# Output gate and z block of each head as a pair with seven-product chunks; the first convolution tap on ScalarE

## The chip, the cores and the metric

The kernel runs on one core of a Trainium2 chip. The metric is the device time of one execution in microseconds, lower is better; before the change it is 1030.87 us, the median of 3 runs from 1030.67 to 1031.13 us.

A core has a matrix engine (TensorE, in the profile PE, with its weight loads as PEld), a vector engine (VectorE, DVE), a scalar engine (ScalarE, ACT), GpSimd (POOL) and SyncE (SP), which here issues the transfers. Each engine takes its instructions in a fixed order and stops at one that waits for a semaphore. Matmuls accumulate in PSUM banks; all other tiles are in SBUF.

## The reference

One residual layer (D = 2048, 256 tokens) with two branches: a bidirectional mLSTM of 4 heads and a bidirectional RG-LRU of 16 blocks. Cut to what the change touches:

```python
# mLSTM branch: q, k, v, o, z are column blocks of one projection of the normalised input
h = h_fwd + h_bwd
h = h * rsqrt(mean(h * h, axis=-1, keepdims=True) + NORM_EPS)
h = h * head_g * sigmoid(o_p) * silu(z_p)

# RG-LRU branch, on the convolution xc (4 taps, 2 to the left) of another column block
r = sigmoid(einsum('bsnc,ncd->bsnd', xb, w_r) + b_r)
i = sigmoid(einsum('bsnc,ncd->bsnd', xb, w_i) + b_i)
a = exp(-LRU_C * r * softplus(-lam))
u = sqrt(-expm1(2.0 * log_a)) * (i * xc)     # then h_t = a_t h_(t-1) + u_t, both ways
```

Both branches are projected to D, merged by sigmoid gates of the input, and projected once more.

## The kernel before

**Numbers.** Every float32 operand x is split into two: a rounded part hi (type fp32r, ACT's cast) and the rest lo = x - hi (DVE). A product is hi·hi + hi·lo + lo·hi, three matmuls.

**Weights.** The weights come in chunks of 128 x 1024 (two rows of tiles of 128, 512 columns each; 512 KB). `load_chunk` (L106) gets a `raw` tile (5 buffers) by a transfer on SP, casts it to `whi` on ACT (L124) and writes `wlo` on DVE (L125), with 4 buffers of `whi` and of `wlo`. `block_nat` (L128) multiplies a block of 512 columns: 8 chunks of 12 matmuls (L139 to L141) into two PSUM banks `acc`. `half_tr` (L268) does half of a block with the result transposed, 4 chunks each with 8 matmuls of 512 columns (L275) and 8 of 256 (L278).

**Pairs.** `pair` (L144), in before used by four later stages, does two column blocks at once. In the chunks listed in `kqs` it replaces the eight block products by seven (Strassen's, in the form of Winograd): `products` (L166) fetches two raw tiles r1 and r2, which the host has stored as sums' parts, makes on DVE the differences t1 (L175, L176) and t2 (L180, L181), splits r1's first half (tile b), t1, t2 and r2 (L160, L161), and issues 21 matmuls in place of 24. The other operand needs a "form", `make_form` (L233): sums of blocks of the activations, split again. The partial results p1, p5, p7, p6 stand in the four `aux` banks, two more pairs of banks are `acc`. After the last product chunk they are joined (L220 to L224), the plain chunks follow, first all of block 0 and then all of block 1 (L225 to L228), each ends with an addition of its `acc` (L230) and an epilogue.

**Heads.** The program runs `rg_block(j)` and `head(j)` for j = 0 to 3 and then the ZB block, four more halves of the same kind as in `rg_block`, and the later stages. `rg_block(j)` (L633) does two `half_tr`, the fold of the result into `xp`, the convolution of 4 channels' groups (L649 first tap, L652 the other three, on DVE), the split of its result into xh (L655) and xl (L656), and puts the LRU's work on a queue. `unit` (L665) is one group's gates in one direction: 6 matmuls with 256 columns into an `aux` bank, two sigmoids (L677), i·xc (L679), a tanh (L681). `decay` (L689) has the 4 exps of a direction, `root` (L697) the two square roots, `scan` (L702) two 1024-wide operations (L704, L705) and four scans (L709 or L711), in direction 1 also the sum (L714).

`head(h)` (L726) does block V (split to vhi and vlo, L733 and L734), block O with a sigmoid from PSUM (L740), block Z with a sigmoid and a product (L745, L746) and the product of both (L747); then `mix` (L753), the product with the mLSTM's weights and the normalisation (L765, L768), and `fin` (L771), four transposes and a split (L782, L783), go on a second queue.

**Order.** Each chunk begins with `tick()` (L89), which takes one entry from each queue: an entry None is a chunk without extra work. So the lists at L716 to L722 and L786 say how many chunks lie between two pieces of work. Within that the tile scheduler orders each engine's instructions by priority; `urgent()` puts loads, casts and evacuations ahead of the rest, and `issue_after` holds a step behind a named instruction.

**Tables on ACT.** ACT loads a table when the function changes from one group to another (rows ACT_TABLE_LOAD); casts and Square need none of their own.

Of the kernel before, what the change touches and what calls it, by code (L numbers as in the profile page):

```python
# [25 lines left out]

S_WB, S_GB, S_GA, S_WA = [((0, 4), (0, 4))] * 4
S_WO = (0, 4)

# [9 lines left out]
def hybrid_encoder(ctx: ExitStack, tc: tile.TileContext, x, xt, pk, bif, fg, wg, wi, wr, wa, wb, wo, out):  # L39
# [12 lines left out]
    def name(n):  # L52
        uid[0] += 1
        return f"{n}_{uid[0]}"
# [88 lines left out]

    def pair(src, xhi, xlo, forms, kqs, dst, b11, epilogue):  # L144
        aps = [aux(i) for i in range(4)]
        p1, p5, p7, p6 = aps
        accs = [acc_pair()[1] for _ in range(2)]
        banks = [[v[:, :NB], v[:, NB:]] for v in accs]
        (d11, d21), (d12, d22) = [(v[:, :NB], v[:, NB:]) for v in dst]
        began = set()  # L150
# [15 lines left out]
        def products(kq, last):  # L166
            lf, rt_ = slice(0, NB), slice(NB, 2 * NB)
            with urgent():
                r1, r2 = [wp.tile([P, KC * NB], F32, tag="raw", name=name("raw"), bufs=5) for _ in range(2)]
                sp.dma_start(r1, src[0][kq])  # L170
                sp.dma_start(r2, src[1][kq])
                b = b11()
                split(b[:, lf], b[:, rt_], r1[:, lf])
                t1 = hp.tile([P, 2 * NB], F32, tag="vhi", name=name("t1"))
# [4 lines left out]
                t2 = hp.tile([P, 2 * NB], F32, tag="vlo", name=name("t2"))  # L179
# [12 lines left out]
            def sf(i):  # L192
                return fm[:, i * P:(i + 1) * P], fm[:, NB + i * P:NB + (i + 1) * P]

            mm(p1, *xb(0, 0), b[:, lf], b[:, rt_], last)
# [17 lines left out]
        for kq in range(last + 1):  # L213
            if kq in kqs:
                products(kq, kq == last)
            else:
                plain(kq, 0)
                plain(kq, 1)
        with urgent():
# [12 lines left out]

    def make_form(fm, full=None, parts=None):  # L233
        u = hp.tile([P, 2 * NB], F32, tag="vhi", name=name("sf"))
        if full is None:
# [397 lines left out]
    def rg_block(j):  # L633
# [31 lines left out]
        def unit(d, n):  # L665
# [10 lines left out]
            for i, v in ((0, av[d]), (1, iv[d])):  # L676
                act.activation(v[:, r], gp[:, i * S:(i + 1) * S], AF.Sigmoid,  # L677
                               bias=pks[:, PK_BRG + d * 2 + i, c:c + 1])
            dve.tensor_mul(iv[d][:, r], iv[d][:, r], xc[:, r])  # L679
            dc = d * KT + c  # L680
            st["a"] = act.activation(tv[d][:, r], av[d][:, r], AF.Tanh, scale=c4[:, dc:dc + 1]).ins  # L681
# [42 lines left out]
    yas = {}  # L724

    def head(h):  # L726
# [8 lines left out]
        to = hp.tile([P, 2 * NB], F32, tag="to", name=name("to"))  # L735
        zz = hp.tile([P, 2 * NB], F32, tag="zz", name=name("zz"))
        ps = block_nat(wi[BLK_O + h], hhi, hlo)
        with urgent():
            for tb in range(2):
                act.activation(to[:, tb * NB:(tb + 1) * NB], ps[tb], AF.Sigmoid)  # L740
        ps = block_nat(wi[BLK_Z + h], hhi, hlo)
        with urgent():
            for tb in range(2):
                v = zz[:, tb * NB:(tb + 1) * NB]
                act.activation(v, ps[tb], AF.Sigmoid)  # L745
                dve.tensor_mul(v, v, ps[tb])  # L746
        dve.tensor_mul(zz, zz, to)  # L747
        sq = hp.tile([P, 2], F32, tag="sq", name=name("sq"), bufs=2)
        if h == 0:
            yas["h"], yas["l"] = sl("A", F32R), sl("B", F32R)  # L750
        yah, yal = yas["h"], yas["l"]

        def mix(tb):  # L753
            num = aux()
# [46 lines left out]
    def h_form(kq, i):  # L801
        h4 = hl_t[:, kq * 4 * S:(kq + 1) * 4 * S].rearrange("p (k q s) -> p k q s", q=2, s=S)
        form("h", kq, i, parts=[h4[:, :, q, :] for q in range(2)])

# [34 lines left out]
    def b11():  # L839
        nb11[0] += 1  # L840
        return hp.tile([P, 2 * NB], F32R, tag=("to", "zz")[nb11[0] % 2], name=name("b11"))

# [129 lines left out]

def _pairs(c, j, kqs):
    for kq in kqs:
        u, v = c[j, kq].copy(), c[j + 1, kq].copy()
        c[j, kq] = np.concatenate([u[:, :NB], v[:, :NB]], axis=1)
        c[j + 1, kq] = np.concatenate([v[:, NB:], u[:, NB:]], axis=1)

# [46 lines left out]
```

## Time and profile before

| | before |
|---|---|
| median of 3 runs | 1030.87 us (1030.67 to 1031.13) |
| profiled run, its span | 1030.37 us, 1028.6 us |
| span outside the profile's first and last instruction | 1.8 us |
| PE busy | 1019.5 us, 99% |
| DVE busy | 786.2 us, 76% |
| ACT busy | 580.1 us, 56% |
| granted clock of PE, mean | 0.998 |
| transfers | 199.32 MB, mean 194 GB/s |

The profiled run is within 0.05% of the median. In the rows of a timeline the first number is the start in microseconds from the first instruction, the second how long the instruction or the run of equal instructions took; matmuls overlap, so their spacing, not their length, is what one costs. In brackets stands the idle time ahead of a row and what ended it. The part "releaser" of such rows is inferred from semaphores.

### The profile page before, as it was taken

Reading aid. Unit: us, or ns where it says so; the run is one execution under the profiler, and the core shown is the slowest. Engines: PE = TensorE matmul, PEld = TensorE weight load, DVE = VectorE, ACT = ScalarE, POOL = GpSimd, SP = SyncE. Lnnn points to the kernel's source line nnn. Section 1 sums busy time; section 2 is a strip of 40 time slices with the busy share of each in tenths; the row PEclk is TensorE's granted clock in tenths of the full one; section 3 lists DMA queues with packets and bytes.
Section 4 is the critical chain, followed back from the end, with each engine's and each line's share of the span. In section 5 each row is a group of like instructions: output and inputs, shape, how many; then the busy total and the mean of one; then the engine's idle time right before and its main releaser. Section 6 shows DMA issues by size and latency. Waiting matters only on the chain.

```text
span 1028.6 us, 13664 instructions
## 1 busy us (share of the span) xinstructions
PE 1019.5 (99%) x5124; PEld 867.3 (84%) x5124; DVE 786.2 (76%) x1039; ACT 580.1 (56%) x763; POOL 11.3 (1%) x35
## 2 busy tenths in 40 slices
PE   9999999999999999999999999999999999999997
PEld 9988888888888888888888888888888888888886
DVE  6787797596578649854977778887787877979784
ACT  7545457745765585559455555545554555454562
POOL 1000000000000000000000000000000000000000
PEclk9999999999999999999999999999999999999999
DMA  9654445554555555554655455555566645666562
GB/s 349 255 188 140 164 162 177 175 203 167 182 201 187 183 179 180 191 190 156 212 184 187 163 203 197 211 209 183 194 204 208 214 167 206 212 244 255 183 205 82
DMA packets 55954, 199.32 MB, mean 194 GB/s; under 512 B 6352, under 2 KB 6864, under 8 KB 55504
## 3 DMA queue, kind: packets, MB, share of 16 engines
q1 hardware_dynamic: 55024, 197.13, 55.1%
q10 hardware_dynamic: 864, 1.32, 0.4%
q8 instruction: 40, 0.66, 0.3%
q14 instruction: 26, 0.21, 0.1%
HBM read 196.33 MB, written 2.10 MB: 193 GB/s over the span
## 4 chain that ended last, share of the span: by engine, by line
PE 98%; DMA 1%; DVE 0%; SPq 0%; ACT 0%; issue 0%; DVEq 0%
PE acc L275 16%; PE acc L157 11%; PE acc L154 11%; PE acc L156 11%; PE acc L139 9%; PE acc L140 9%; PE acc L141 9%; PE acc L278 8%; PE aux L154 2%; PE aux L157 2%; PE aux L156 2%; PE aux L761 1%; PE aux L675 1%; PE aux L674 1%; PE aux L673 1%; PE aux L951 1%
## 5 line engine op out<-in xcount | busy, mean ns | idle before, releaser
L125 DVE TENSOR_TENSOR wlo<-raw,whi 128x1024 fp32r<-128x1024 f32 (+1 forms) x321 | 389.3, 1219 | 154.6 <-ACT whi L124 152.6
L124 ACT CAST whi<-raw 128x1024 fp32r<-128x1024 f32 (+1 forms) x321 | 334.4, 1048 | 267.7 <-PE acc L141 80.9
L275 PE MATMUL acc<-sHL,whi 128*128 128x512 f32 x704 | 178.6, 394 | 0.0
L139 PE MATMUL acc<-whi,sHL 128*128 128x512 f32 x416 | 162.4, 390 | 0.0
L140 PE MATMUL acc<-wlo,sHL 128*128 128x512 f32 x416 | 162.2, 390 | 0.0
L141 PE MATMUL acc<-whi,sHL 128*128 128x512 f32 x416 | 162.0, 389 | 0.0
L275 PEld LDWEIGHTS acc<-sHL,whi 128*128 128x128 f32 x704 | 127.0, 189 | 23.7
L278 PEld LDWEIGHTS acc<-sHL,wlo 128*128 128x128 f32 x704 | 96.1, 190 | 7.2
L156 PE MATMUL acc<-wlo,sHL 128*128 128x512 f32 x260 | 101.1, 389 | 0.0
L157 PE MATMUL acc<-whi,sHL 128*128 128x512 f32 x260 | 101.1, 389 | 0.0
L154 PE MATMUL acc<-whi,sHL 128*128 128x512 f32 x260 | 99.5, 389 | 0.0
L278 PE MATMUL acc<-sHL,wlo 128*128 128x256 f32 x704 | 99.2, 283 | 0.0
L141 PEld LDWEIGHTS acc<-whi,sHL 128*128 128x128 f32 x416 | 78.1, 188 | 16.3
L139 PEld LDWEIGHTS acc<-whi,sHL 128*128 128x128 f32 x416 | 78.2, 188 | 15.6
L140 PEld LDWEIGHTS acc<-wlo,sHL 128*128 128x128 f32 x416 | 78.2, 188 | 15.3
L160 ACT CAST whi<-t 128x1024 fp32r<-128x1024 f32 x36 | 37.9, 1053 | 57.4 <-PE acc L157 41.2
L157 PEld LDWEIGHTS acc<-whi,sHL 128*128 128x128 f32 x260 | 48.8, 188 | 10.2
L156 PEld LDWEIGHTS acc<-wlo,sHL 128*128 128x128 f32 x260 | 48.8, 188 | 10.2
L154 PEld LDWEIGHTS acc<-whi,sHL 128*128 128x128 f32 x260 | 48.8, 188 | 10.1
L161 DVE TENSOR_TENSOR wlo<-t,whi 128x1024 fp32r<-128x1024 f32 x36 | 44.0, 1223 | 14.6 <-ACT whi L160 14.6
L156 PE MATMUL acc<-wlo,sA 128*128 128x512 f32 x104 | 40.6, 390 | 0.0
L157 PE MATMUL acc<-whi,sB 128*128 128x512 f32 x104 | 40.5, 390 | 0.0
(314 smaller groups left out, 1435.2 us busy)
## 6 DMA issues: line engine op xcount, KB each, us to landing
raw<-wi SPq DMA_DIRECT2D x255, 512.0 KB, 3.6
raw<-wb SPq DMA_DIRECT2D x32, 512.0 KB, 3.7
raw<-wa SPq DMA_DIRECT2D x32, 512.0 KB, 3.7
raw<-wo SPq DMA_DIRECT2D x32, 512.0 KB, 4.4
raw<-wr SPq DMA_DIRECT2D x8, 512.0 KB, 3.6
sB<-x SPq DMA_DIRECT2D x4, 512.0 KB, 8.3
sA<-x SPq DMA_DIRECT2D x1, 2048.0 KB, 7.4
sA<-xt SPq DMA_DIRECT2D x7, 256.0 KB, 7.2
```

The costliest lines, as they stand in the source:

```text
L124: last_copy[0] = act.copy(hi[:, r], raw[:, r]).ins
L125: last_sub[0] = dve.tensor_sub(lo[:, r], raw[:, r], f(hi[:, r])).ins
L139: pe.matmul(ps[tb], a, wh, start=(k == 0), stop=False)
L140: pe.matmul(ps[tb], a, wl, start=False, stop=False)
L141: pe.matmul(ps[tb], b, wh, start=False, stop=(k == KT - 1))
L154: pe.matmul(ps, a, wh, start=id(ps) not in began, stop=False)
L156: pe.matmul(ps, a, wl, start=False, stop=False)
L157: pe.matmul(ps, b, wh, start=False, stop=stop)
L160: act.copy(hi, v)
L161: dve.tensor_sub(lo, v, f(hi))
L275: pe.matmul(ps[m], hi[:, o:o + P], hl_t[:, 2 * k * S:2 * (k + 1) * S], start=(k == 0), stop=False, skip_group_check=True)
L278: pe.matmul(ps[m][:, :S], lo[:, o:o + P], hhi(k * S, (k + 1) * S), start=False, stop=(k == KT - 1), skip_group_check=True)
```

## The change

1. In `head`, blocks O and Z are done by `pair`, with product chunks 0, 2 and 4 in heads 0, 1 and 2, and 0 and 2 in head 3 (`S_OZ`); the other chunks are plain. t1 and t2 use the tiles of `to` and `zz`. The sigmoids and products of O and Z become the epilogue `epi_oz`, on whole tiles in SBUF: sigmoid(o) when block O is done; when Z is done, o·z, sigmoid(z) and their product.
2. The three forms of the input that this needs are made once, in head 0, ahead of its block V; they lie in free parts of the tiles that later hold the head outputs. Tile b has a place of its own.
3. The convolution's first tap is an ACT activation with scale and bias. xl is written by one subtraction over 1024 columns, after all four groups; i·xc by one product a direction, after its second pair of units.
4. The LRU's queue entries are fewer: the units of direction 1 and the decays, root and scans have other due chunks.
5. On the host the columns of O and Z are stored as the pair needs them; the number of bytes is the same.

```diff
+S_OZ = ((0, 2, 4), (0, 2, 4), (0, 2, 4), (0, 2))
...
-    def pair(src, xhi, xlo, forms, kqs, dst, b11, epilogue):
+    def pair(src, xhi, xlo, forms, kqs, dst, b11, epilogue, tmp=("vhi", "vlo")):
...
-            dve.tensor_scalar(v, xp[:, n, 0:S], pks[:, PK_CW, c:c + 1], pks[:, PK_CB, c:c + 1],
-                              op0=ALU.mult, op1=ALU.add)
+            act.activation(v, xp[:, n, 0:S], AF.Identity, scale=pks[:, PK_CW, c:c + 1], bias=pks[:, PK_CB, c:c + 1])
...
             act.copy(xh[:, r], v)
-            dve.tensor_sub(xl[:, r], v, f(xh[:, r]))
+        dve.tensor_sub(xl, xc, f(xh))
...
-            dve.tensor_mul(iv[d][:, r], iv[d][:, r], xc[:, r])
...
             unit(d, 2 * half + 1)
+            if half:
+                dve.tensor_mul(iv[d], iv[d], xc)
...
-            queue.extend([None] * (5 if d == 0 else 4))
+            queue.extend([None] * (5 if d == 0 else 1))
             for half in range(2):
                 queue.append(lambda d=d, half=half: gates(d, half))
-        queue.extend([None, None])
-        queue.extend([lambda: decay(0), None, lambda: decay(1), None, root, None, None, lambda: scan(0), None,
-                      lambda: scan(1)])
+        queue.extend([None, lambda: decay(0), lambda: decay(1), root, None, lambda: scan(0), None, lambda: scan(1)])
...
+        if h == 0:
+            yas["h"], yas["l"] = sl("A", F32R), sl("B", F32R)
+            for kq, (t, i) in ((0, ("h", 3)), (2, ("l", 3)), (4, ("h", 2))):
+                hf[kq] = yas[t][:, i * 1024:(i + 1) * 1024]
+                make_form(hf[kq], parts=h_parts(kq), tag="to" if kq % 4 else "zz")
...
-        ps = block_nat(wi[BLK_O + h], hhi, hlo)
-        with urgent():
-            for tb in range(2):
-                act.activation(to[:, tb * NB:(tb + 1) * NB], ps[tb], AF.Sigmoid)
-        ps = block_nat(wi[BLK_Z + h], hhi, hlo)
-        with urgent():
-            for tb in range(2):
-                v = zz[:, tb * NB:(tb + 1) * NB]
-                act.activation(v, ps[tb], AF.Sigmoid)
-                dve.tensor_mul(v, v, ps[tb])
-        dve.tensor_mul(zz, zz, to)
+        def epi_oz(jj):
+            to, zz = dst
+            if jj == 0:
+                act.activation(to, to, AF.Sigmoid)
+            else:
+                dve.tensor_mul(to, to, zz)
+                act.activation(zz, zz, AF.Sigmoid)
+                dve.tensor_mul(zz, zz, to)
...
+        pair((wi[BLK_O + h], wi[BLK_Z + h]), hhi, hlo, hf, S_OZ[h], dst, b11, epi_oz, tmp=("to", "zz"))
```

The order of the instructions moves with it. Three places follow; the names carry running numbers (whi_2962 is one buffer's use), and in the changed kernel the lines are later by one to fifteen: casts L125, wlo L126, gates L679 (sigmoid) and L682 (tanh), exp L697, root L703, scan L707, L708, L712, L714.

ACT in head 1, before, from the last gate unit of direction 1 to the first cast behind the sigmoid of block O:

```order
L124 CAST whi_2774<-raw_2773 128x1024
L677 ACTIVATE sC_468_2385<-aux_2704,pks 128x256
L677 ACTIVATE sC_470_2387<-aux_2704,pks 128x256
L681 ACTIVATE sD_471_2388<-sC_468_2385,c_175 128x256 x2
L694 ACT_TABLE_LOAD
L694 ACTIVATE sC_467_2384<-sC_467_2384,c_174 128x256 x4
L124 CAST whi_2795<-raw_2794 128x1024
L694 ACTIVATE sC_468_2385<-sC_468_2385,c_174 128x256 x4
L124 CAST whi_2817<-raw_2816 128x1024
L124 CAST whi_2835<-raw_2834 128x1024
L700 ACT_TABLE_LOAD
L700 ACTIVATE sE_1520<-sE_1520 128x1024
```

The same place of ACT in the changed kernel, from the load for the exps; the last unit's sigmoids (on aux_2898) stand behind it:

```order
L697 ACT_TABLE_LOAD
L697 ACTIVATE sC_484_2431<-sC_484_2431,c_174 128x256 x4
L697 ACTIVATE sC_485_2432<-sC_485_2432,c_174 128x256 x3
L125 CAST whi_2984<-raw_2983 128x1024
L703 ACT_TABLE_LOAD
L703 ACTIVATE sE_1520<-sE_1520 128x1024
L125 CAST whi_3004<-raw_3003 128x1024
L679 ACT_TABLE_LOAD
L679 ACTIVATE sC_485_2432<-aux_2898,pks 128x256
L679 ACTIVATE sC_487_2434<-aux_2898,pks 128x256
L125 CAST whi_3028<-raw_3027 128x1024
L682 ACTIVATE sD_488_2435<-sC_485_2432,c_175 128x256
```

Seven of the eight exps and the first root run ahead of the last unit, so behind its tanh come the sigmoid of O, a load and the eighth exp, a load and the second root, and a load for the sigmoid of Z.

DVE at the transition from head 1 to the RG block of head 2, changed kernel, from the first scan step:

```order
L707 SCALAR_TENSOR_TENSOR sE_1520<-sC_484_2431,sE_1520 128x1024
L126 TENSOR_TENSOR wlo_3068<-raw_3066,whi_3067 128x1024
L708 TENSOR_TENSOR sE_1520<-sE_1520,sC_486_2433 128x1024
L126 TENSOR_TENSOR wlo_3101<-raw_3099,whi_3100 128x1024
L707 SCALAR_TENSOR_TENSOR sD_488_2435<-sC_485_2432,sD_488_2435 128x1024
L712 SCALAR_TENSOR_TENSOR sE_1520<-sC_484_2431,sE_1520 128x256 x4
L233 TENSOR_TENSOR zz_2848<-zz_2848,acc_2639 128x1024
L126 TENSOR_TENSOR wlo_3130<-raw_3128,whi_3129 128x1024
L708 TENSOR_TENSOR sD_488_2435<-sD_488_2435,sC_487_2434 128x1024
L126 TENSOR_TENSOR wlo_3156<-raw_3154,whi_3155 128x1024
L753 TENSOR_TENSOR to_2847<-to_2847,zz_2848 128x1024
L126 TENSOR_TENSOR wlo_3187<-raw_3185,whi_3186 128x1024
```

In before these scan steps stood in block Z; now they stand with the joins of the pair (L233, L753) between the wlo of the next RG block's chunks.

DVE at the start of the pair of head 0, changed kernel, from the joined xl (L658): vlo (L745), the third form (L245 to L250), i·xc (L690) and the first product chunk's t1, t2, b (L161 to L181):

```order
L658 TENSOR_TENSOR sD_290_1527<-sD_288_1525,sD_289_1526 128x1024
L745 TENSOR_TENSOR vlo_1581<-acc_1582,vhi_1580 128x512
L245 TENSOR_TENSOR sf_1572<-sf_1572 128x128
L247 TENSOR_TENSOR sf_1572<-sf_1572 128x128
L161 TENSOR_TENSOR wlo_1794<-t_355_1790,whi_1793 128x1024
L246 TENSOR_TENSOR sf_1572<-sf_1572 128x128
L745 TENSOR_TENSOR vlo_1581<-acc_1582,vhi_1580 128x512
L248 TENSOR_TENSOR sf_1572<-sf_1572 128x128
L690 TENSOR_TENSOR sC_293_1551<-sC_293_1551,sD_288_1525 128x1024
L250 TENSOR_TENSOR sA_1554<-sf_1572,sA_1554 128x512
L161 TENSOR_TENSOR sB_1555<-raw_1865,sB_1555 128x512
L180 TENSOR_TENSOR t_358_1797<-t_355_1790,raw_1784 128x512
```

None of these but the xl, i·xc and vlo has a counterpart there in before; t2 (L180) and its split now stand behind i·xc, which waits for the last sigmoid of direction 0.

More of the change, by code (lines that the diff above doesn't have):

```diff
@@ L171, in products @@
                 sp.dma_start(r2, src[1][kq])
-                b = b11()
-                split(b[:, lf], b[:, rt_], r1[:, lf])
-                t1 = hp.tile([P, 2 * NB], F32, tag="vhi", name=name("t1"))
+                bh, bl = b11()
+                split(bh, bl, r1[:, lf])
+                t1 = hp.tile([P, 2 * NB], F32, tag=tmp[0], name=name("t1"))
                 dve.tensor_sub(t1[:, lf], r1[:, rt_], r1[:, lf])
@@ L193, in sf @@
                 return fm[:, i * P:(i + 1) * P], fm[:, NB + i * P:NB + (i + 1) * P]
-            mm(p1, *xb(0, 0), b[:, lf], b[:, rt_], last)
+            mm(p1, *xb(0, 0), bh, bl, last)
             mm(p5, *sf(0), h1[:, lf], l1[:, lf], last)
@@ L218, in pair @@
                 plain(kq, 1)
+        if not dst:
+            dst.extend(hp.tile([P, 2 * NB], F32, tag=t, name=name(t)) for t in ("to", "zz"))
+        (d11, d21), (d12, d22) = [(v[:, :NB], v[:, NB:]) for v in dst]
         with urgent():
@@ L231, in pair, with make_form @@
                 epilogue(jj)
-    def make_form(fm, full=None, parts=None):
-        u = hp.tile([P, 2 * NB], F32, tag="vhi", name=name("sf"))
+    def make_form(fm, full=None, parts=None, tag="vhi"):
+        u = hp.tile([P, 2 * NB], F32, tag=tag, name=name("sf"))
         if full is None:
@@ L716, in rg_block, with h_parts @@
         for d in range(2):
-            queue.extend([None] * (5 if d == 0 else 4))
+            queue.extend([None] * (5 if d == 0 else 1))
             for half in range(2):
                 queue.append(lambda d=d, half=half: gates(d, half))
-        queue.extend([None, None])
-        queue.extend([lambda: decay(0), None, lambda: decay(1), None, root, None, None, lambda: scan(0), None,
-                      lambda: scan(1)])
+        queue.extend([None, lambda: decay(0), lambda: decay(1), root, None, lambda: scan(0), None, lambda: scan(1)])
     yas = {}
+    hf = {}
+    def h_parts(kq):
+        h4 = hl_t[:, kq * 4 * S:(kq + 1) * 4 * S].rearrange("p (k q s) -> p k q s", q=2, s=S)
+        return [h4[:, :, q, :] for q in range(2)]
     def head(h):
+        if h == 0:
[3 more added lines that the diff above has]
+                make_form(hf[kq], parts=h_parts(kq), tag="to" if kq % 4 else "zz")
         vhi = hp.tile([P, 2 * NB], F32R, tag="vhi", name=name("vhi"))
@@ L801, in h_form @@
     def h_form(kq, i):
-        h4 = hl_t[:, kq * 4 * S:(kq + 1) * 4 * S].rearrange("p (k q s) -> p k q s", q=2, s=S)
-        form("h", kq, i, parts=[h4[:, :, q, :] for q in range(2)])
+        form("h", kq, i, parts=h_parts(kq))
     def ya_form(kq, i):
@@ L840, in b11 @@
         nb11[0] += 1
-        return hp.tile([P, 2 * NB], F32R, tag=("to", "zz")[nb11[0] % 2], name=name("b11"))
+        v = hp.tile([P, 2 * NB], F32R, tag=("to", "zz")[nb11[0] % 2], name=name("b11"))
+        return v[:, :NB], v[:, NB:]
     sgb = sl("E")
@@ L970, in _chunks, with _pairs @@
         w.reshape(KT // KC, KC, P, n, NB).transpose(3, 0, 2, 1, 4).reshape(n, KT // KC, P, KC * NB))
-def _pairs(c, j, kqs):
+def _pairs(c, j, kqs, n=1):
     for kq in kqs:
-        u, v = c[j, kq].copy(), c[j + 1, kq].copy()
+        u, v = c[j, kq].copy(), c[j + n, kq].copy()
         c[j, kq] = np.concatenate([u[:, :NB], v[:, :NB]], axis=1)
-        c[j + 1, kq] = np.concatenate([v[:, NB:], u[:, NB:]], axis=1)
+        c[j + n, kq] = np.concatenate([v[:, NB:], u[:, NB:]], axis=1)
 def _halves(w):
@@ L999 @@
     _pairs(wo, 0, S_WO)
+    for h in range(NH):
+        _pairs(wi, BLK_O + h, S_OZ[h], BLK_Z - BLK_O)
     cols = [v.reshape(-1, KT, P) for v in (a["norm_g"][0][None], a["head_g"][0][None], a["conv_b"][0][None],
```

15 lines of the change are left out of this document (8 added, 7 removed).

## The prediction

> **What bounds the kernel now.** I read the page's head first, then the waits of PE, then windows.
>
> ```profile
> span 1028.6 us, 13664 instructions
> PE 1019.5 (99%) x5124; PEld 867.3 (84%) x5124; DVE 786.2 (76%) x1039; ACT 580.1 (56%) x763; POOL 11.3 (1%) x35
> ...
> PE aux L305 <- DVE wu L337: 1.1, 1, 1.1
> PE acc L265 <- DVE wlo L125: 0.8, 1, 0.8
> ```
>
> PE is busy in 1019.5 of 1028.6 us, and only two of its waits are listed, 1.9 us in all, both in the first microseconds. So every matmul that goes is worth its full issue time, and every wait that PE is given is paid in full. The windows show how much room the other engines have. The columns are the stretch, its length, then busy time of PE, PEld, DVE and ACT.
>
> ```profile
> core 0: us, PE busy (x) PEld busy (x) DVE busy (x) ACT busy (x) POOL busy (x), PEclk, DMA share, GB/s
> 137.30:161.50 24.20, 24.20 (x118) 20.24 (x117) 22.10 (x37) 14.86 (x23) 0.00 (x0) 1.00 0.48 165
> 307.10:404.20 97.10, 97.10 (x486) 82.61 (x485) 68.92 (x89) 61.14 (x91) 1.66 (x4) 1.00 0.54 184
> 307.10:332.50 25.40, 25.40 (x147) 22.32 (x146) 22.68 (x33) 13.98 (x22) 1.66 (x4) 1.00 0.55 188
> 358.40:382.50 24.10, 24.10 (x119) 20.43 (x118) 12.79 (x15) 19.15 (x32) 0.00 (x0) 1.00 0.50 172
> 598.00:690.00 92.00, 92.00 (x408) 76.17 (x407) 77.64 (x90) 47.49 (x51) 0.00 (x0) 1.00 0.59 206
> 1010.00:1029.00 19.00, 11.34 (x95) 11.13 (x93) 6.84 (x19) 2.54 (x6) 0.00 (x0) 0.86 0.30 111
> ```
>
> One head with its RG block takes 97.1 us. Over the whole of it DVE and ACT have slack, but not in its parts: DVE is at 22.7 of 25.4 us in the RG block and at 22.1 of 24.2 in the first V block, ACT at 19.2 of 24.1 where the LRU gates end. What hides this is the lead of the weight tiles: four whi/wlo pairs, some four chunks ahead of PE.
>
> **The saving.** Two matmul rows, 11 issues apart with nothing else between, give the price.
>
> ```profile
> 334.17 0.39 PE L140 MATMUL acc<-wlo,sHL 128*128 128x512 f32 x1
> ...
> 336.66 0.39 PE L139 MATMUL acc<-whi,sHL 128*128 128x512 f32 x1
> ```
>
> (336.66 - 334.17)/11 = 0.226 us for a 128x512 matmul; a plain chunk of 12 is 2.7 us. A product chunk does the two chunks of both matrices with 21 matmuls in place of 24. There are 3 + 3 + 3 + 2 = 11 of them, so 33 matmuls go: 33 x 0.226 = **-7.5 us**. It is certain, since PE is the bound. All the rest is whether PE still never waits.
>
> **What ACT gets.** The rows of the pinch in head 1 give its prices: start, duration, line.
>
> ```profile
> 370.75 0.83 ACT L677 ACTIVATE sC<-aux,pks 128x256 f32<-128x256 f32 x2
> 371.48 1.05 ACT L124 CAST whi<-raw 128x1024 fp32r<-128x1024 f32 x1
> ...
> 373.13 0.92 ACT L681 ACTIVATE sD<-sC,c 128x256 f32<-128x256 f32 x2
> 374.07 1.28 ACT L694 ACT_TABLE_LOAD   x1
> 375.36 1.71 ACT L694 ACTIVATE sC<-sC,c 128x256 f32<-128x256 f32 x4
> 376.98 1.04 ACT L124 CAST whi<-raw 128x1024 fp32r<-128x1024 f32 x1
> 377.92 1.71 ACT L694 ACTIVATE sC<-sC,c 128x256 f32<-128x256 f32 x4
> ...
> 381.54 1.28 ACT L700 ACT_TABLE_LOAD   x1
> 382.83 1.06 ACT L700 ACTIVATE sE<-sE 128x1024 f32<-128x1024 f32 x1
> 383.80 1.04 ACT L700 ACTIVATE sD<-sD 128x1024 f32<-128x1024 f32 x1
> 384.84 1.28 ACT L740 ACT_TABLE_LOAD   x1
> ...
> 387.11 1.05 ACT L124 CAST whi<-raw 128x1024 fp32r<-128x1024 f32 x1
> ```
>
> From start to start: table load 1.29, exp 0.41, sigmoid 0.37, tanh 0.46, cast 0.95, square root 0.97. Before, a head has three loads: Exp, Sqrt, Sigmoid. In the changed order it has six (the last gate unit's Sigmoid comes after Exp and Sqrt and needs both again), that is 12 more over the kernel, 15.5 us of ACT. It stands in a stage that begins with the gates of direction 1, which now lie in the tail of the pair, and it is serial. Added up over the changed rows from the cast ahead of the third gate unit to the cast of whi_3067: 5 casts (4.8), 5 loads (6.5), 8 exps (3.3), 2 roots (1.9), 4 sigmoids and 2 tanhs (2.4), the 1024-wide sigmoid (1.0) = 19.9 us, in which PE uses up 7 chunks while only 5 are cast. The lead falls by two chunks. DVE, which needs these casts and roots, stands idle in it for some 12 us and has its work afterwards.
>
> The Trainium skill, "ScalarE: Activation LUTs", section "What ACT_TABLE_LOAD costs", puts a drain of 1.38 us behind each load's 1.28. The rows disagree: the first exp starts 1.29 us after its load. By the page the five loads would make the stretch 6.9 us longer, and the transitions about 2 us each dearer, some 8 us in all.
>
> **What DVE has to catch up.** Prices from the same place of before:
>
> ```profile
> 388.19 3.50 DVE L125 TENSOR_TENSOR wlo<-raw,whi 128x1024 fp32r<-128x1024 f32 x3 [5.23 <-ACT whi L124]
> 391.60 1.22 DVE L704 SCALAR_TENSOR_TENSOR sE<-sC,sE 128x1024 f32<-128x1024 f32 x1
> ...
> 395.13 2.43 DVE L709 TENSOR_TENSOR_SCAN sE<-sC,sE 128x256 f32<-128x256 f32 x4
> 397.48 1.20 DVE L125 TENSOR_TENSOR wlo<-raw,whi 128x1024 fp32r<-128x1024 f32 x1
> ...
> 407.73 0.69 DVE L746 TENSOR_TENSOR zz<-zz,acc 128x512 f32<-128x512 f32 x1
> 408.33 1.22 DVE L125 TENSOR_TENSOR wlo<-raw,whi 128x1024 fp32r<-128x1024 f32 x1
> ```
>
> A 1024-wide operation costs 1.14 us back to back, four scans 2.35, a 512-wide one 0.60. Here DVE also waits 5.2 us for ACT and then works without a gap, and PE is not held up: but all of it lies in the Z block, with plain chunks of 2.7 us and no more than one step of the scans between two wlo. In the changed order the same catch-up stands ahead of and inside the next RG block, where DVE was at 22.7 of 25.4 us already, with the joins of the pair (L233 twice, L753, L755) put in: 8 wlo, 4 operations of L707/L708, 8 scans, L233, L753, L755, L717, a fold and two L781 are 16 x 1.14 + 4.7 + 0.6 + 1.4 = about 24 us, against 20 us of PE work up to fin's transposes. Walking both queues down from the root PE meets wlo_3130 about 1.5 us late, as it stands behind L707, four scans and L233; wlo_3240 0.3 late; and the transposes of fin, which wait for L781, 1.7 late. **Three transitions at 3.5 us = 10.5** (2 to 5 each). At head 3, where the ZB block follows, the same walk gives 2.0 at the first wlo behind the scans, 0.4, and 1.5 at fin: **3.9** (1.5 to 5).
>
> **The start of head 0.**
>
> ```profile
> L242 DVE TENSOR_TENSOR sf<-sf 128x128 f32<-128x128 f32 x6 | 1.7, 290 | 0.1
> ...
> 153.22 1.28 ACT L677 ACT_TABLE_LOAD   x1
> 154.51 1.57 ACT L677 ACTIVATE sC<-aux,pks 128x256 f32<-128x256 f32 x4
> ...
> raw<-wi SPq DMA_DIRECT2D x255, 512.0 KB, 3.6
> ```
>
> In V0 DVE has 2.1 us free, and gets three forms (one 512-wide sum, four of 128, one 512-wide rest: 0.6 + 4 x 0.29 + 0.6 = 2.4 us each) and the first t1. V ends at 137.3 + 96 x 0.226 + 2 gate products and 8 transposes, about 160.2. xl, now one operation, is written about 161.3, and 22 of 24 gate matmuls stand behind it: 1.1 us. The banks of the products p1, p5 and p7 are the gates' own, so these wait for eight sigmoids, two tanhs and the table load: behind the casts of vhi and t1, from 162.3, 1.29 + 8 x 0.37 + 2 x 0.46 = 5.2 bring the last to 167.5. DVE's queue then has L690, which waits for it (1.14), the form's rest (0.6), b (0.6), L180 and L181 (0.6 each), to 171.2; ACT casts h2 by 172.4. Without waits PE would start p6 at 165.6: 6.8 us. The second r2 reuses the raw that L180 lets go, so it lands at 170.6 + 3.6 = 174.3, L176 waits for it on DVE, and l3 stands behind L176: 1.6 more at the next products. **Head 0: +8.4** (5 to 10). None of this is hidden: the products are next in PE's queue. In heads 1 to 3 the forms exist and half the gates are done earlier; there the second r2 (also behind L180) leaves 0.4 each: **+1.2** (0 to 3).
>
> **Edits that cost nothing here.** The first tap on ACT is 16 activations of at most 0.5 us in RG blocks where ACT is busy for 14.0 of 25.4 us; it takes as many short operations off DVE. The joined iv product and xl save DVE the starts of some short operations. If that cover were gone, the taps would cost at most 16 x 0.5 = 8 us, if DVE's relief were all on the path, as much the other way; I take 0, since the LRU's input is folded a chunk or more before the gates need it and DVE's relief is in the walk. The wr loads keep their bytes, and at 0.54 of DMA time there is room.
>
> **Sum.** 1028.6 + 1.8 around the span is the profiled run of 1030.4, against the median of 1030.9. Waits 8.4 + 10.5 + 1.2 + 3.9 = 24.0; net 24.0 - 7.5 = +16.5, so 1046.9. The walk charges each wait to its latest producer and lets no gain from one wait (a refilled lead) run into the next; I take 1.9 off for that, and say **1045.0**. All low ends: 5 + 6 + 0 + 1.5 = 12.5, 1035.4; all high: 10 + 15 + 3 + 5 = 33, 1055.9.
>
> **Rivals.** (a) *The lead covers all.* In before ACT is held from 370.8 to 387.1 and DVE idles 5.2 us, yet PE never waits, so four pairs bear a stretch of 16 us. If the new stretch stays under four chunks, 4 x 2.7 = 11 us of lag, and head 0's banks come free in time, only the saving is left: 1030.4 - 7.5 = 1022.9. Against it: the lag at 390 was already within about 1 us of PE (the first of the three wlo that start at 388.19 is ready at 389.4, and by the count of chunks PE reads it from about 390.5), and there is more work now. It decides if fin's transposes and wlo_3130 are not in PE's waits. 0.12. (b) *Only head 0.* Its wait needs no lag, just the order of the queues: 1030.4 - 7.5 + 8.4 = 1031.3. 0.08. (c) *A clock that drops.* The granted clock is 1.00 in every window but the last, where PE is busy 11.3 of 19 us and it is 0.86. If head 0's waits, pieces of 1 to 3 us within 12, do the like for 20 us, 0.14 x 20 = 3 us come on top: 1048. 0.15. The Trainium skill, "TensorE: Matmul & The Clock Gate", section "HAM oscillation — how this bites in real kernels", lets the clock fall after idle gaps above about 3.4 us; my longest piece is below that, so by the page nothing falls.
>
> **Chances.** Forecast (waits of 12 to 33 us) 0.65, (c) 0.15, (b) 0.08, (a) 0.12. A difference under 0.2%, 2 us, can't be told from none. Faster 0.13, same 0.08, slower 0.79. The range leaves out (a) and a little of the top: 1031 to 1055.
>
> **What would show it.** PE's waits after: a group before the products of head 0, for ACT or DVE, 6 us or more in all; wlo waits behind the scans in each RG block; L789 waiting for L781. The period of a head near 99 us in place of 97.1 (9 matmuls less, 2.0; waits of 3.9 more). PE's busy time lower by 7.5. Wrong, if PE's waits stay under 5 us: then the lead is longer than I walked, and the time falls below 1030.

## The result and the profile after

The changed kernel takes 1057.13 us (median of 4 runs, 1055.24 to 1058.43), the kernel before 1030.77 us beside it: 1.0256 of it, 95% interval 1.024 to 1.0271. It is slower by 26.4 us; the forecast was slower by 14.

The page of the changed kernel begins:

```profile
span 1056.6 us, 13706 instructions
PE 1025.1 (97%) x5091; PEld 861.3 (82%) x5091; DVE 844.1 (80%) x1091; ACT 623.1 (59%) x812; POOL 17.0 (2%) x35
```

The 33 matmuls are gone (5124 to 5091 instructions of PE), and still PE is busy for 5.6 us longer. Its idle time went from 9.1 us (1028.6 - 1019.5) to 31.5. Of the profiled run's 28.0 us of longer span, that is 22.4 us of idle time and 5.6 of busy time in place of the 7.5 that should have gone. Busy time hides a part of the loss: a matmul right behind a wait (0.50 us long) or on a lower clock (0.63) counts as busy for longer than its 0.39 us.

The waits of PE, where before had two rows with 1.9 us:

```profile
PE aux L789 <- DVE to L781: 5.3, 5, 1.4
PE acc L156 <- DVE wlo L126: 5.2, 5, 1.5
PE acc L281 <- DVE wlo L126: 4.0, 3, 1.3
PE aux L154 <- ACT sC L679: 2.0, 3, 1.7
PE acc L156 <- DVE wlo L161: 1.9, 4, 0.6
PE aux L154 <- ACT whi L160: 1.7, 1, 1.7
```

Row 3 and three of the waits of row 1 are the transitions from a head to the next RG block; the other two of row 1 are head 3's transposes in the ZB block (0.8 and 0.2). Rows 4 and 6 are the start of head 0. Rows 2 and 5 are mostly the first products of heads 1 to 3; two of the waits of row 2 (0.3 and 1.5) are the last plain chunks of head 3, ahead of the ZB block, and one of row 5 (0.4) is head 0's.

The windows of head 0's first products and of the first products of head 3 (busy time of PE, PEld, DVE, ACT, POOL, then the granted clock):

```profile
core 0: us, PE busy (x) PEld busy (x) DVE busy (x) ACT busy (x) POOL busy (x), PEclk, DMA share, GB/s
165.00:172.50 7.50, 4.12 (x12) 1.94 (x12) 4.12 (x7) 5.51 (x15) 0.00 (x0) 0.97 0.02 4
173.00:179.00 6.00, 5.66 (x13) 4.14 (x14) 5.24 (x6) 4.18 (x5) 0.00 (x0) 0.50 0.38 128
480.00:482.00 2.00, 1.12 (x4) 0.59 (x4) 2.00 (x3) 0.90 (x2) 0.00 (x0) 1.00 0.52 168
482.00:487.00 5.00, 4.75 (x14) 3.77 (x15) 3.67 (x5) 0.97 (x2) 0.00 (x0) 0.66 0.84 299
```

In two places the clock falls behind PE's waits: to 0.50 from 173 to 179 us, with 13 matmuls where 26 would fit, and to 0.66 from 482 to 487.

Where the time came from can be read from the starts of the RG blocks. They are the first matmul of `half_tr` (L275 before, L278 after) in PE's timeline:

```profile
221.28 1.98 PE L278 MATMUL acc<-sHL,whi 128*128 128x512 f32 x8
...
322.18 1.98 PE L278 MATMUL acc<-sHL,whi 128*128 128x512 f32 x8
...
423.30 1.98 PE L278 MATMUL acc<-sHL,whi 128*128 128x512 f32 x8
...
526.84 0.61 PE L278 MATMUL acc<-sHL,whi 128*128 128x512 f32 x2
```

A head with its RG block took 97.1 us before, and 100.9, 101.1 and 103.5 us now. With 9 matmuls fewer (2.0 us) it should take 95.1, so heads 1 and 2 lose 5.8 to 6.1 us each. The sizes of single losses below are spacings of PE's starts less 0.227 us for each 128x512 matmul and 0.119 for each 128x256; they include the 0.15 to 0.3 us by which the row of a wait is too short.

| place | forecast, us | measured, us |
|---|---|---|
| start of head 0, waits | 8.4 | 7.2 |
| three transitions to the next RG block | 10.5 | 3.6 each, 10.9 |
| product starts of heads 1 to 3 | 1.2 | 1.8, 2.0, 2.1: 5.8 |
| head 3 to ZB | 3.9 | 3.9 |
| lower clock | none (rival c: 3) | 2.7 in head 0, 1.6 in head 3 |
| the rest: 0.7 ahead of head 0, pieces under 0.3 us | none | 3.4 |
| sum | 24.0 | 35.5 (28.0 + 7.5) |

The start of head 0, as DVE has it after the change:

```profile
164.83 0.28 DVE L248 TENSOR_TENSOR sf<-sf 128x128 f32<-128x128 f32 x1
168.45 1.22 DVE L690 TENSOR_TENSOR sC<-sC,sD 128x1024 f32<-128x1024 f32 x1 [3.35 <-ACT sC L679]
169.60 0.68 DVE L250 TENSOR_TENSOR sA<-sf,sA 128x512 fp32r<-128x512 f32 x1
170.20 0.68 DVE L161 TENSOR_TENSOR sB<-raw,sB 128x512 fp32r<-128x512 f32 x1
170.80 0.69 DVE L180 TENSOR_TENSOR t<-t,raw 128x512 f32<-128x512 f32 x1
171.52 0.69 DVE L181 TENSOR_TENSOR t<-raw,t 128x512 f32<-128x512 f32 x1
```

Row 2, L690, the joined i·xc, waits 3.35 us for the last sigmoid, and everything that the next products need stands behind it. ACT has t2's cast ready at 173.3, and PE starts p6 at that time:

```profile
173.34 0.80 PE L154 MATMUL aux<-whi,sA 128*128 128x512 f32 x1 [1.67 <-ACT whi L160]
173.94 0.63 PE L154 MATMUL acc<-whi,sHL 128*128 128x512 f32 x1
...
176.16 0.63 PE L157 MATMUL acc<-whi,sHL 128*128 128x512 f32 x1
176.59 0.63 PE L154 MATMUL acc<-whi,sHL 128*128 128x512 f32 x1
```

Here the spacing of two matmuls is 0.43 us in place of 0.23, which is the lower clock.

The end of head 1 on ACT:

```profile
314.66 1.03 ACT L125 CAST whi<-raw 128x1024 fp32r<-128x1024 f32 x1
315.70 1.28 ACT L679 ACT_TABLE_LOAD   x1
317.00 0.84 ACT L679 ACTIVATE sC<-aux,pks 128x256 f32<-128x256 f32 x2
317.73 1.05 ACT L125 CAST whi<-raw 128x1024 fp32r<-128x1024 f32 x1
318.67 0.52 ACT L682 ACTIVATE sD<-sC,c 128x256 f32<-128x256 f32 x1
319.08 1.05 ACT L751 ACTIVATE to<-to 128x1024 f32<-128x1024 f32 x1
320.14 1.28 ACT L697 ACT_TABLE_LOAD   x1
321.43 0.51 ACT L697 ACTIVATE sC<-sC,c 128x256 f32<-128x256 f32 x1
321.95 1.28 ACT L703 ACT_TABLE_LOAD   x1
323.24 1.06 ACT L703 ACTIVATE sD<-sD 128x1024 f32<-128x1024 f32 x1
```

Three loads of 1.28 us serve one gate unit, one exp and one root. The next cast starts at 324.2, 6.5 us after the one at 317.73. DVE has nothing from 321.4 to 325.3 and meets the RG block late. PE waits there at a wlo behind four scans and at fin:

```profile
334.55 1.21 PE L281 MATMUL acc<-sHL,wlo 128*128 128x256 f32 x8 [1.34 <-DVE wlo L126]
...
348.36 0.44 PE L789 MATMUL aux<-ident,to 128*128 128x128 f32 x2 [1.42 <-DVE to L781]
```

### The profile page after: what moved, and what is told of

Its sections match the earlier page's. It is cut to its first block, busy times and chain, and to the rows that moved or that the text cites. A ratio compares the mean times of both kernels' runs of the same rounds, so it can differ in the third digit from the quotient of the medians.

```text
span 1056.6 us, 13706 instructions
## 1 busy us (share of the span) xinstructions
PE 1025.1 (97%) x5091; PEld 861.3 (82%) x5091; DVE 844.1 (80%) x1091; ACT 623.1 (59%) x812; POOL 17.0 (2%) x35
## 4 chain that ended last, share of the span: by engine, by line
PE 62%; DVE 11%; issue 3%; ACT 2%; DMA 1%; POOL 0%; DVEq 0%; POOLq 0%; ACTq 0%
PE acc L156 13%; PE acc L157 13%; PE acc L154 13%; PE acc L278 6%; PE acc L281 3%; DVE wlo L126 3%; PE aux L156 2%; PE aux L157 2%; PE aux L154 2%; PE acc L140 1%; PE acc L142 1%; PE acc L141 1%; DMA raw<-wi 1%; DVE sC L714 1%; DVE sD L654 1%
## 5 line engine op out<-in xcount | busy, mean ns | idle before, releaser
L126 DVE TENSOR_TENSOR wlo<-raw,whi 128x1024 fp32r<-128x1024 f32 (+1 forms) x299 | 362.2, 1215 | 106.0 <-ACT whi L125 104.8
L125 ACT CAST whi<-raw 128x1024 fp32r<-128x1024 f32 (+1 forms) x299 | 309.9, 1047 | 188.5 <-PE acc L157 74.0
L278 PE MATMUL acc<-sHL,whi 128*128 128x512 f32 x704 | 178.9, 394 | 0.0
L157 PE MATMUL acc<-whi,sHL 128*128 128x512 f32 x450 | 176.3, 392 | 0.0
L154 PE MATMUL acc<-whi,sHL 128*128 128x512 f32 x450 | 174.3, 392 | 0.0
L278 PEld LDWEIGHTS acc<-sHL,whi 128*128 128x128 f32 x704 | 126.8, 189 | 24.0 <-ACT whi L125 0.8
L156 PEld LDWEIGHTS acc<-wlo,sHL 128*128 128x128 f32 x450 | 85.2, 189 | 29.3 <-DVE wlo L126 8.3
L160 ACT CAST whi<-t 128x1024 fp32r<-128x1024 f32 x58 | 61.1, 1053 | 78.7 <-PE acc L157 42.8
L154 PEld LDWEIGHTS acc<-whi,sHL 128*128 128x128 f32 x450 | 85.3, 190 | 17.7
L157 PEld LDWEIGHTS acc<-whi,sHL 128*128 128x128 f32 x450 | 85.2, 189 | 17.3
L161 DVE TENSOR_TENSOR wlo<-t,whi 128x1024 fp32r<-128x1024 f32 x58 | 70.5, 1220 | 16.1 <-ACT whi L160 15.8
L140 PE MATMUL acc<-whi,sHL 128*128 128x512 f32 x160 | 62.6, 391 | 0.0
L142 PE MATMUL acc<-whi,sHL 128*128 128x512 f32 x160 | 62.5, 390 | 0.0
L161 DVE TENSOR_TENSOR wlo<-raw,whi 128x1024 fp32r<-128x1024 f32 x29 | 35.5, 1223 | 21.1 <-ACT whi L160 21.0
L160 ACT CAST whi<-raw 128x1024 fp32r<-128x1024 f32 x29 | 30.5, 1052 | 25.7 <-PE acc L157 23.1
L154 PE MATMUL acc<-whi,sA 128*128 128x512 f32 x111 | 43.4, 395 | 0.0
```

The source lines that it names most:

```text
L125: last_copy[0] = act.copy(hi[:, r], raw[:, r]).ins
L126: last_sub[0] = dve.tensor_sub(lo[:, r], raw[:, r], f(hi[:, r])).ins
L140: pe.matmul(ps[tb], a, wh, start=(k == 0), stop=False)
L142: pe.matmul(ps[tb], b, wh, start=False, stop=(k == KT - 1))
L154: pe.matmul(ps, a, wh, start=id(ps) not in began, stop=False)
L156: pe.matmul(ps, a, wl, start=False, stop=False)
```

## The experiments

Twelve kernels were run, each against the kernel before on the same chip.

Of the runs e_, three change one thing in the changed kernel and e_small puts one part of the change on the kernel before. The runs c_ combine corrections of the changed kernel.

| run | time, us | ratio to before (95%) |
|---|---|---|
| the change | 1057.13 | 1.0256 (1.024 to 1.0271) |
| e_h0plain: plain first chunk in head 0 | 1047.76 | 1.017 (1.0155 to 1.0185) |
| e_order: exps and roots held | 1042.68 | 1.0126 (1.0107 to 1.0144) |
| e_unjoin: xl, i·xc by group | 1050.82 | 1.0195 (1.018 to 1.021) |
| e_small: small edits alone, on before | 1030.59 | 0.9999 (0.999 to 1.0009) |
| c_h0_order | 1035.79 | 1.0048 (1.0034 to 1.0063) |
| c_h0_order_unjoin | 1034.96 | 1.0041 (1.0028 to 1.0054) |
| c_late_order | 1040.72 | 1.0099 (1.0085 to 1.0113) |
| c_late_order_unjoin | 1034.85 | 1.0038 (1.0026 to 1.0051) |
| c_t2 | 1031.35 | 1.001 (1.0001 to 1.0018) |
| c_wide | 1032.84 | 1.0022 (1.0014 to 1.0031) |
| c_one | 1031.74 | 1.0012 (1.0003 to 1.0021) |
| c_best | 1031.98 | 1.0013 (1.0004 to 1.0022) |

### Head 0 without products in its first chunk

```diff
-S_OZ = ((0, 2, 4), (0, 2, 4), (0, 2, 4), (0, 2))
+S_OZ = ((2, 4), (0, 2, 4), (0, 2, 4), (0, 2))
```

> The changed kernel with plain first chunks of O and Z in head 0 (products only at chunks 2 and 4 there). Theory (the start of head 0 is held by the gates' banks and by the order of DVE's queue, and the stall then drops the clock): the 7.2 us of waits of PE between 161 and 191 us fall to 0 to 2, the granted clock stays at 1.00 from 160 to 200 us, 3 matmuls come back (0.7): the time falls by 7 to 10 us. Rival (the first products stall wherever they stand, since their raw tiles and t2 are late): the waits move to chunk 2 and the time falls by less than 3 us.

It took 9.4 us off. Windows of this run, at head 0 and at the transition behind it:

```profile
160.00:200.00 40.00, 38.40 (x191) 32.50 (x190) 32.34 (x40) 30.24 (x49) 0.00 (x0) 1.00 0.57 181
220.00:232.00 12.00, 9.52 (x48) 8.12 (x47) 12.00 (x16) 5.77 (x6) 0.00 (x0) 0.86 0.39 133
```

PE idles 1.6 us in the 40 us of head 0's start (one wait for the gates' sigmoids, before chunk 2), and the clock there is 1.00. The theory holds. What was not expected: the clock now falls at the first transition, where DVE is busy all 12 us and PE waits 2.5 us at one wlo, so this gain is measured with a new loss in it.

### Exps behind all tanhs, roots behind all exps

```diff
+            st.setdefault("t", []).append(st["a"])
...
-            with tc.issue_after(st["a"]), tc.issue_after(last_copy[0]):
+            with ExitStack() as es:
+                for i in st["t"] + [st["a"], last_copy[0]]:
+                    es.enter_context(tc.issue_after(i))
...
+                    st.setdefault("e", []).append(i.ins)
...
-            with tc.issue_after(st["a"]), tc.issue_after(last_copy[0]):
+            with ExitStack() as es:
+                for i in st["e"] + [last_copy[0]]:
+                    es.enter_context(tc.issue_after(i))
```

The condition in the changed kernel names one tanh, that of the unit written last. The unit that uses p5's bank, the last of the four to come free, is not that one; it comes later on ACT, so the exps pass ahead of it.

> The changed kernel with the exps held behind all tanhs and the roots behind all exps: three table loads a head in place of six. Theory (the loads hold ACT, so DVE idles and then has its work late): ACT's loads fall by 12 x 1.28 = 15.4 us, the waits of PE at the wlo behind the scans and at fin, 3.6 us a transition, fall to 0 to 1.5 each, the time falls by 5 to 11 us. Rival (DVE's 24 us of work against 20 of PE decide by themselves): the waits at the wlo and at fin stay above 3 us a transition and the time falls by less than 2 us.

It took 14.5 us off, more than expected, and is the largest cause. ACT's table loads in the heads, by group of instructions, in this run:

```profile
L700 ACT ACT_TABLE_LOAD x4 | 5.1, 1283 | 0.1
L709 ACT ACT_TABLE_LOAD x4 | 5.1, 1283 | 0.0
L757 ACT ACT_TABLE_LOAD x4 | 5.1, 1283 | 0.1
```

The waits of PE in this run from 200 to 320 us, a whole head with both of its transitions, are one row:

```profile
PE acc L156 <- DVE wlo L126: 1.1, 1, 1.1
```

It is that of a product start. The waits at a wlo behind the scans and at fin are gone, and a head now takes 97.2 us. DVE's work is all still there (busy 843.9 us against 844.1), so the rival, that it is too much by itself, falls for this place. Measured from the same cast of head 1, ACT is through with the second root 2.3 us earlier, and DVE's idle 3.9 us behind its first scan step are gone. The order on DVE moved with it (two wlo now stand together behind the second L707); how much of the gain is that order's was not tried apart. The spans of the two profiled executions differ by more than the medians, 16.5 us (1056.6 - 1040.1): the clock's fall in head 3 is not in this one either.

### xl and i·xc by group

```diff
-        dve.tensor_sub(xl, xc, f(xh))
+            dve.tensor_sub(xl[:, r], v, f(xh[:, r]))
...
-            if half:
-                dve.tensor_mul(iv[d], iv[d], xc)
+            dve.tensor_mul(iv[d][:, r], iv[d][:, r], xc[:, r])
```

> The changed kernel with xl and i*xc written group by group again, as before the change. Theory (the joined i*xc waits for the last sigmoid and holds the wlo and t2 behind it on DVE at the start of each pair): the waits at the product starts fall from 1.8 to 2.1 us to about 0.7 in heads 1 to 3, head 0's by 1 to 3 us: the time falls by 3 to 7 us. Rival (they are late because the second product's raw tiles land late): the waits of heads 1 to 3 stay within 0.5 us, and the more DVE operations add 0 to 2 us.

It took 6.3 us off. The product starts of heads 1 to 3 fell from 5.8 us together to about 2.2 (0.5, 1.7 and nothing over 0.25), head 0's start from 7.2 to about 6.5. Its waits at fin grew:

```profile
PE aux L788 <- DVE to L780: 6.9, 5, 2.0
PE aux L154 <- ACT whi L160: 3.9, 1, 3.9
```

In head 0 the waits didn't go away but met in one, of 3.9 us, for t2's cast. The wlo waits behind the scans are 0.2 each here, in place of 1.3. The theory of the joined operation holds in heads 1 and 3, not in head 2, where 1.3 us stay at the plain chunk's wlo. The rival, late raw tiles, is not out by this: they come late here too, and DVE waits for them for 1.1 to 2.0 us ahead of the first plain chunks of each pair, against 2.5 to 2.8 in the changed kernel.

### The small edits alone

```diff
-            dve.tensor_scalar(v, xp[:, n, 0:S], pks[:, PK_CW, c:c + 1], pks[:, PK_CB, c:c + 1],
-                              op0=ALU.mult, op1=ALU.add)
+            act.activation(v, xp[:, n, 0:S], AF.Identity, scale=pks[:, PK_CW, c:c + 1], bias=pks[:, PK_CB, c:c + 1])
...
+        dve.tensor_sub(xl, xc, f(xh))
...
+                dve.tensor_mul(iv[d], iv[d], xc)
```

> The kernel before with only the small edits: the first tap on ACT, joined xl and joined i*xc; O and Z, and the queue, as before. Theory (the small edits are free by themselves): within 1 us of the kernel before, no wait of PE over 0.5 us. Rival (the joins stall gates or scans): PE waits for xl or i*xc, 2 to 6 us slower.

No difference. The same joined operations cost 6 us in the changed kernel and nothing here, where no product stands behind them on DVE.

### Both corrections, and the joins undone

> The two corrections together: plain first chunks in head 0 and the exps and roots held behind the whole set ahead of them. Theory (the two causes are separate, 9.4 and 14.5 us): 1057.1 - 9.4 - 14.5 = 1033.3, 1031 to 1036. Rival (they share one resource, the lead of the weight tiles, so one correction takes part of the other's gain): 1037 or more.

> The same with xl and i*xc group by group. Theory (of the 6.3 us that this gave by itself, the share in head 0 and at fin is gone, the product starts of heads 1 to 3 remain, 5.8 us to 2.2): 2 to 4 us below the run without it, about 1030. Rival (DVE's further operations cost what the starts gain): the same time within 1 us.

1035.79: the two gains add to 21.3 us of the 23.9 of the single runs, so the causes are nearly separate. Undoing the joins gave 0.8 us more (less than the 2 to 4 expected; the intervals of the two ratios overlap). What is left stands mostly at the product starts of heads 1 to 3, 1.3 to 2.0 us each, and at those of head 0, 1.8.

### Products only at chunks 2 and 4

```diff
+S_OZ = ((2, 4),) * 4
...
-            for kq, (t, i) in ((0, ("h", 3)), (2, ("l", 3)), (4, ("h", 2))):
+            for kq, (t, i) in ((2, ("l", 3)), (4, ("h", 2))):
```

> Exps and roots held as above, and products only at chunks 2 and 4 in all four heads (8 product chunks, 24 matmuls fewer than before: 5.4 us); the form for chunk 0 is not made. Theory (a first chunk with products is what finds its tiles late): no wait over 0.5 us at a product start, 1030.6 - 5.4 + 1 to 3 = 1026 to 1029, faster than the kernel before. Rival (two products in three chunks overload DVE wherever they stand): waits of 1 us or more at each second product, 1030 or more.

> The same with xl and i*xc group by group. Theory (with the products late, i*xc has time, joined or not): within 1 us of the run with the joins. Rival: 2 us or more faster, then the joined i*xc still holds the plain chunks' wlo.

In both runs head 2's outputs have taken the place of the form that head 3 multiplies by at chunk 4, so these kernels leave head 3's right output out; the amount of work is the same. Both expectations missed: 1040.72 with the joins, 1034.85 without, 5.9 us apart, so the joins matter here too. With the joins heads 1 and 2 lose 0.7 and 1.2 us at the plain chunks' tiles and head 3 2.8, without them head 2 0.7 and head 3 1.7. The rest is new, at the ZB block: with its product at chunk 4 head 3 has its joins later, and PE waits 2.1 us there for the fold (L293) behind them, with the joins also 1.6 us at fin. The clock falls behind these waits in both runs (0.55 from 535 to 540 us with the joins, 0.66 from 530 to 535 without). A product moved away from the start of the pair was late at its end.

### t2 of the next product behind the plain chunks

The run c_h0_order_unjoin with this edit in `products`:

```diff
+                with ExitStack() as es:
+                    if kq and kq - 1 not in kqs and tmp[0] == "to":
+                        es.enter_context(tc.issue_after(last_sub[0]))
+                    dve.tensor_add(t2[:, lf], t1[:, rt_], r1[:, lf])
+                    dve.tensor_sub(t2[:, rt_], r2[:, rt_], t2[:, lf])
```

> The run with both corrections and without the joins (1034.96 us), with t2 of a later product chunk held behind the wlo of the plain chunks ahead of it. Theory (at the product starts of heads 1 to 3 the plain chunk's wlo stands on DVE behind t2, 0.6 us, and is 1.1 us late): that wait falls to 0.6 or less each, the time falls by 1.5 to 3.5 us. Rival (the order only moves the delay to the next product): the waits at the plain chunk's wlo fall and as much comes back at the second product's split, the same within 1 us or slower.

It took 3.6 us off, a little more than expected, and the waits of PE at the plain chunks' wlo of heads 1 to 3 are 0.5 each in place of 1.1 (the fourth of the row is head 0's):

```profile
PE acc L156 <- DVE wlo L126: 2.2, 4, 0.6
```

The rows of the changed kernel show why, here at the start of head 2's pair:

```profile
372.15 0.69 DVE L175 TENSOR_TENSOR t<-raw 128x512 f32<-128x512 f32 x1 [1.64 <-DMA raw<-wi]
373.93 0.69 DVE L176 TENSOR_TENSOR t<-raw,raw 128x512 f32<-128x512 f32 x1 [1.08 <-DMA raw<-wi]
374.54 1.22 DVE L161 TENSOR_TENSOR wlo<-t,whi 128x1024 fp32r<-128x1024 f32 x1
375.68 1.22 DVE L690 TENSOR_TENSOR sC<-sC,sD 128x1024 f32<-128x1024 f32 x1
376.81 0.68 DVE L180 TENSOR_TENSOR t<-t,raw 128x512 f32<-128x512 f32 x1
377.41 1.22 DVE L161 TENSOR_TENSOR wlo<-raw,whi 128x1024 fp32r<-128x1024 f32 x1
378.55 0.68 DVE L181 TENSOR_TENSOR t<-raw,t 128x512 f32<-128x512 f32 x1
379.15 0.68 DVE L745 TENSOR_TENSOR vlo<-acc,vhi 128x512 fp32r<-128x512 f32 x1
379.75 1.21 DVE L126 TENSOR_TENSOR wlo<-raw,whi 128x1024 fp32r<-128x1024 f32 x1
```

PE needs the last of these and starts on it at 381.02. Ahead of it stand i·xc (1.14) and t2 (1.2), which nobody waits for yet. The first two rows are t1 of the second product: DVE waits there 2.7 us for its raw tiles, with the first product's l2 and l3 (the two rows of L161) behind it, and then works without a gap. That landing is the rival that stays open. No run changed it alone; c_t2 and e_unjoin gained with the raw tiles still late, so the order on DVE has a share, but an earlier landing might have covered the same loss.

### Fewer products

c_wide has products at chunks 0 and 4 in heads 1 and 2, c_one has a single one in each head (chunk 4, in head 3 chunk 2), both on c_h0_order_unjoin.

> The same run (1034.96 us) with the products of heads 1 and 2 at chunks 0 and 4 only (8 product chunks in all, 24 matmuls fewer than before; two product chunks fewer than in that run, 1.4 us back). Theory (the second product's raw tiles and t1, t2 crowd the first plain chunks): the waits at the starts of heads 1 and 2, 1.3 to 2.0 us, fall below 0.7 each: 1032.5 to 1035. Rival (they belong to the first product): the waits stay and the time is 1035.5 to 1037.

> The same run with one product chunk a head (chunk 4 in heads 0 to 2, chunk 2 in head 3; 12 matmuls fewer than before, 2.7 us; two forms made). Theory (only the crowd of products costs, the pair itself is free once ACT's order is mended): waits of PE within 1.5 us of before's, 1028.5 to 1030, faster than the kernel before by 0.6 to 2 us. Rival (the pair itself, its joins on SBUF tiles and the scans in the next RG block, costs some 3 us or more): 1031 or more.

c_wide came as expected; waits over 0.3 us at the starts of heads 1 and 2 are gone, where the second product's raw tiles and its t1 and t2 have gone together, and head 3 keeps its 2.3. c_one went with its rival: 2.7 us of matmuls were saved and the time is 1.2 us above before, so a pair costs about 1 us a head even with one product. Its waits are fin's (1.1 us each with what follows, at three transitions) and one of 0.9 some 8 us into head 3's pair.

### The best pieces together

Products at 2 and 4, 0 and 4, 0 and 4, 0 and 2, t2 held, and the form for chunk 0 made in head 1.

> All corrections (order of exps and roots, no joins, t2 held behind the plain chunks), products at chunks 2 and 4 in head 0, 0 and 4 in heads 1 and 2, 0 and 2 in head 3 (24 matmuls fewer than before, 5.4 us), the form for chunk 0 made in head 1. Worked out from the stages of the other runs: head 0 with two forms made took 72.4 us (the run with products at 2 and 4), heads 1 and 2 with products at 0 and 4 took 96.6 each against 97.1 before, head 3 with t2 held 96.0: 361.5 against 363.9 before, so 1028 to 1029.5, faster than the kernel before by 1 to 2.5 us. Rival (the third form, now in head 1, costs there what it cost in head 0, 2 us, or the pieces don't add): 1030 to 1032.

1031.98, the rival's range: the pieces don't add. Head 1, with the third form, took 98.4 us where 96.6 was expected, close to the 2 us that the rival named; heads 2 and 3 took 96.6 and 96.2, as expected. The busy times of its page:

```profile
PE 1017.2 (99%) x5100; PEld 861.4 (84%) x5100; DVE 834.8 (81%) x1109; ACT 601.4 (58%) x794; POOL 14.4 (1%) x35
```

PE is busy for 2.3 us less than before where 24 matmuls, 5.4 us, are gone. The largest group of its waits is still fin's, the mix of which (L789 here) comes late on DVE:

```profile
PE aux L797 <- DVE to L789: 1.3, 3, 0.5
```

No version tried is faster than the kernel before. Three (c_t2, c_one, c_best) are within 0.2% of it.

## Why the prediction was wrong

The direction was right, and so were the places and mechanisms of the two largest terms; the time lies 2 us above the range. The profiled execution lost 35.5 us where the forecast, after its 1.9 us for slack, had 22.1. The 13.4 us between them are 4.6 at the product starts, 4.3 of lower clock, 3.4 of small pieces and the 1.9, less 0.8 by which the other terms were too high. By its steps:

- **The saving** of 7.5 us is there in the count of instructions (33 fewer). The sign named for it, PE's busy time lower by 7.5, did not come: it is higher by 5.6, as late and slow matmuls count as busy.
- **ACT and the transitions.** Forecast 10.5 + 3.9, measured 10.9 + 3.9, at the instructions named (the wlo behind four scans, fin's transposes). e_order shows the cause: with the order mended these waits are gone. Its 14.5 us are near the sum of both, 14.8, though the clock moved too. The walk's "about 24 us" of DVE work adds up to 24.9, which changes nothing in this.
- **The start of head 0.** Forecast p6 at 172.4 us, measured 173.3, with the V block 0.7 later; the waits are 7.2 us for 8.4. Shown by e_h0plain, which also took the clock's fall away there.
- **The step that failed** is "there the second r2 (also behind L180) leaves 0.4 each: **+1.2** (0 to 3)", the product starts of heads 1 to 3. They cost 1.8 to 2.1 us each, 5.8 together. What the step had in mind is there: the second r2 is late, and l3, behind L176 and then i·xc and half of t2, holds PE for 0.5 to 0.8 us. What it left out is larger: 1.3 us in each head at the plain chunk's wlo. The walk looked at when the second product's tiles land and not at what DVE does between that landing and the plain chunk's wlo. e_unjoin (i·xc) and c_t2 (t2) each took a part of it away; how much an earlier landing would take is open. The upper end of that term, 3, was too low as well.
- **The clock** was kept out of the sum, as a rival with a chance of 0.15 and 3 us. It fell twice in the profiled execution, 2.7 and 1.6 us, so that rival came true on top of the forecast. The high ends of the sum, 1055.9, held no such term. The four runs agree with its size: those with a mean granted clock of 0.993 and 0.991 took 1058.4 us, those with 0.996 and 0.995 took 1055.2 and 1055.9.
- **The 1.9 us taken off** for slack had the wrong sign. 3.4 us are left that the walk didn't have, 0.7 of them ahead of head 0 and the others in small pieces. Where those come from wasn't tried.

The period of heads 1 and 2 shows the same step: forecast near 99 us, measured 100.9 and 101.1, and the product starts cost 1.4 to 1.6 us more in each than forecast.

That the small edits cost nothing was right by themselves (e_small) but not in their place: the joined i·xc was priced as a saving of DVE time, and its cost is what stands behind it.

## What to carry to other kernels

A matmul saved at a bound of 99% is worth 0.23 us at most, and the pairs buy the 33 with 23 more 1024-wide and 69 more 512-wide operations on DVE (counted in the two traces, without the 12 that join xl and i·xc), which feeds PE; price the stages where those land, not the average of 76%. An operation that is joined to save starts takes the latest of its inputs, and everything behind it on its engine waits for that too. When a step must follow a set of instructions, hold it behind all of them: here one tanh of eight was named, and twelve table loads came of it.

## What was not expected of the hardware

The granted clock fell to half behind short waits. In the changed kernel no wait of PE is longer than 1.7 us, and it was 0.50 from 173 to 179 us, after 7.5 us in which PE was busy 4.1, and 0.66 from 482 to 487, after 2 us in which it was busy 1.1. Heads 1 and 2 have much the same waits at the same place (0.3 and 0.5 us, then 1.1 each; head 3 has 0.6 and 1.1) and kept their clock at 1.00. In e_order head 3 has a longer pair, 0.8 and 1.1 us, and its clock is 1.00 too. The Trainium skill, "TensorE: Matmul & The Clock Gate", section "HAM oscillation — how this bites in real kernels", speaks of idle gaps above about 3.4 us; no wait of the changed kernel was that long, and the clock fell all the same. What decides it, the runs don't settle.
